# One float32 comparison for both one-hot sets of the gate rows, and a written TensorE order in block 2

## The chip, the cores and the metric

The kernel runs on one core of a Trainium2 chip. The metric is the device time of one execution in microseconds (us). The engines are TensorE (PE, with its weight loads as PEld), VectorE (DVE), ScalarE (ACT), GpSimd (POOL) and SyncE (SP), which issues most of the transfers. Each engine works through its own instructions in a fixed order and waits on semaphores for the others.

## The reference, cut to what matters

The program is two transformer blocks over 512 tokens of 1024 channels, in float32. The first is a hybrid attention layer, which the change does not touch. The second has a token mixer (here called block 2) and a PEER layer:

```
p = xn @ w_in                      # 7 column groups: xa ga vb bb cb ma mb
ya = rg_lru(conv4(xa) + b) * gelu(ga)
yb = bb * conv3(cb * vb)
h  = h + (sigmoid(ma) * ya + sigmoid(mb) * yb) @ w_out
...
idx, g = top-16 of 256 candidates, for 8 heads and each token   # 128 experts of 16384
act = gelu(u[idx] . xn);   out = sum over the 128 of g * act * v[idx]
```

rg_lru has two gates, each a 128x128 matmul per head on the convolved xa, and a scan over the tokens.

## The kernel before

**Numbers.** Large matmuls are done as three: weights and inputs are split into a high part (a cast by ACT, `whi`, `xhi`) and the rest (a subtraction, `wlo`, `xlo`), and hi*hi, lo*hi and hi*lo are summed in PSUM. A weight block of 128 columns is loaded by SP (`wraw`), cast by ACT and subtracted by POOL or DVE; each of the three has a ring of 3.

**Block 2** (`block2`) runs over 8 blocks of 128 channels. Each takes seven tiles of 24 matmuls, in the order xa, ga, vb, bb, cb, ma, mb, which `next_tile` makes and which alternate between two PSUM buffers (`mm`). The first three tiles of the first block (`ahead`) are made at the end of block 1, while its sums come in. `scaled` multiplies a tile by the row of norms `rb` on DVE, which also empties the PSUM buffer. From xa comes the convolution `xc` (one ACT and three DVE operations), split into `xch` and `xcl`, on which `gates` does twice three matmuls (`pr`, `pi`). Their tanh leads by ACT, DVE and POOL to the scan `hs`. At the end `mhi` and `mlo` hold the merged channels, and eight output tiles over `wo2` (k is a channel block) are added to the residual `mo` (the variable `xr`). `RmsSum` takes their squares: `add` sums them on DVE and, for the last two, gives them to PE as matmuls with a column of ones (`st`).

The order of each engine's instructions is set by the scheduler of the framework from its own estimates. The code's order is a preference only.

**Gate rows** (`gate_matrix`). Token group 0 is done by gathering rows. For the groups 1, 2 and 3 (`DT`) all 16384 experts are computed densely, and a matrix of gates is needed: for each token, row (128) by column (128) of the expert number. Per 128 tokens, indices and weights are transposed on PE (`gt`), the index is cut in two 7-bit halves (`hi_`, `iT`), and then for each 4 tokens: two DVE comparisons make one-hot rows in bfloat16,

```
eq = R.tile([128, 2, 128, 4], BF16, name="eq", bufs=2)
for e in range(2):
    V.tensor_tensor(out=eq[:, e], in0=iota, in1=iT[:, e, None, t:t + 4].to_broadcast([128, 128, 4]),
                    op=OP.is_equal)
```

ACT copies the first set to float32 (`A`), POOL multiplies the second by the weights (`B`), PE multiplies the two for each of the 4 tokens in float32 (`gp`, 4 matmuls, 8 records in the trace), and ACT copies the result to `stage`. 8 such groups of 4 tokens make one transfer of 2 MB to `gd` in DRAM; 3 x 128 tokens are 96 groups.

**Around it.** `u_step` loads a block of 128 rows of u, splits it and multiplies it with the 384 tokens (`ups`, 24 matmuls), DVE scales it (`act`), ACT takes the gelu. 11 of these are written into `peer_query`, the others into `peer_experts`, and the scheduler pulls some of them among the gate rows. After the gate rows `peer_experts` goes through all 128 blocks: remaining u steps, gates read back (`gate<-gd`), and 18 matmuls for v (`acc`).

Of the kernel before, what the change touches and what calls it, by code (L numbers as in the profile page):

```python
# [6 lines left out]
F32 = mybir.dt.float32  # L7
# [10 lines left out]
KD = 8  # L18
# [747 lines left out]
def block2(g, xr):  # L766

    nc, tc = g.nc, g.tc
    V = nc.vector
    with ExitStack() as ctx:  # L770
        P = ctx.enter_context(tc.tile_pool(name="b2", bufs=1, reuse_waits="tile"))
        R = ctx.enter_context(tc.tile_pool(name="b2r", bufs=2, reuse_waits="tile"))
        pb = g.pg
# [12 lines left out]
        def next_tile():  # L786
            return ahead.pop(0) if ahead else emit_tile()

        mhi = P.tile([128, 8, T], F32R, name="mhi")
        mlo = P.tile([128, 8, T], F32R, name="mlo")  # L790
        def scaled(nm, out=None, half=False):
            t = out if out is not None else R.tile([128, T], F32, name=nm)
            if half:
                V.scalar_tensor_tensor(t, next_tile(), 0.5, rb, op0=OP.mult, op1=OP.mult)
            else:
                V.tensor_tensor(out=t, in0=next_tile(), in1=rb, op=OP.mult)
            return t

        for i in range(8):
# [18 lines left out]
            def gates(o, e):  # L818
                for j, (w, x) in enumerate(((wah, xch), (wal, xch), (wah, xcl))):
                    nc.tensor.matmul(o, w[:, e, :], x, start=j == 0, stop=j == 2)  # L820

            gates(pr, 0)
            tr = t("tr")
            nc.scalar.activation(tr, pr, AF.Tanh, scale=0.5, bias=bh[:, i:i + 1])
# [15 lines left out]
            hs = t("hs", "xc")  # L840
            V.tensor_tensor_scan(hs, av, ti, 0.0, op0=OP.mult, op1=OP.add)

            ga = scaled("ga")
            g2 = t("g2")
            nc.scalar.activation(g2, ga, AF.Square)
            V.tensor_scalar(out=g2, in0=g2, scalar1=GC, scalar2=1.0, op0=OP.mult, op1=OP.add)
# [2 lines left out]
            V.scalar_tensor_tensor(g2, g2, 1.0, ga, op0=OP.add, op1=OP.mult)  # L849
            nc.gpsimd.tensor_tensor(out=hs, in0=hs, in1=g2, op=OP.mult)  # L850

            vb = scaled("vb")
            bb = scaled("bb")
            cb = R.tile([128, 2 + T], F32, name="cb")
            nc.gpsimd.memset(cb[:, 0:2], 0.0)
# [18 lines left out]

        g.xhi, g.xlo, g.rb, g.rtok = operands(g)
        st = RmsSum(g, R, "pt")
        for k in range(KD):
            ps = proj_tile(g, wblock(g, g.a["wo2"][k]), mhi, mlo)
            V.tensor_tensor(out=xr[:, k, :], in0=ps, in1=xr[:, k, :], op=OP.add)
            scaled_split(g, g.xhi, g.xlo, xr, "n2", [k])  # L880
            st.square(xr[:, k, :])
            st.add()
        st.finish(g.rb, g.rtok)


# [6 lines left out]
GPAD = 128  # L892
NEXP = 128
RUN = 32
GB = 3
ULO = 10
NROW = 4
SMH = 4
# [127 lines left out]
def gate_matrix(g, gd):  # L1026

    nc, tc = g.nc, g.tc
    V = nc.vector
    nb = 0  # L1030
    with tc.tile_pool(name="peg", bufs=2, reuse_waits="tile") as R:
        iota = R.tile([128, 128, 4], BF16, name="iota", bufs=1)
        nc.gpsimd.tensor_copy(iota, g.cst[:, C_IOTA:C_IOTA + 128, None].to_broadcast([128, 128, 4]))
        for m, tt in enumerate(DT):
            ps = g.pg.tile([128, 512], F32, name="gt", tag="pg")
            nc.tensor.transpose(ps[:, 0:128], g.idxf[:, tt, :], g.ident)
            nc.tensor.transpose(ps[:, 128:256], g.wgt[:, tt, :], g.ident)
            ii = R.tile([128, 128], I32, name="ii", bufs=1)
            V.tensor_copy(ii, ps[:, 0:128])
            wT = R.tile([128, 128], F32, name="wT")  # L1040
            nc.scalar.copy(wT, ps[:, 128:256])
            hi_ = R.tile([128, 2, 128], I32, name="hi_", bufs=1)
            V.tensor_scalar(out=hi_[:, 0, :], in0=ii, scalar1=7, scalar2=None, op0=OP.logical_shift_right)
            V.tensor_scalar(out=hi_[:, 1, :], in0=ii, scalar1=127, scalar2=None, op0=OP.bitwise_and)
            iT = R.tile([128, 2, 128], BF16, name="iT")
            V.tensor_copy(iT, hi_)
            for b in range(128 // TB):
                stage = R.tile([128, 128, TB], F32, name="stage")
                for q in range(TB // 4):
                    t = b * TB + q * 4  # L1050
                    eq = R.tile([128, 2, 128, 4], BF16, name="eq", bufs=2)
                    for e in range(2):
                        V.tensor_tensor(out=eq[:, e], in0=iota, in1=iT[:, e, None, t:t + 4].to_broadcast([128, 128, 4]),  # L1053
                                        op=OP.is_equal)
                    A = R.tile([128, 4, 128], F32, name="A", bufs=GB)
                    nc.scalar.copy(A, eq[:, 0].rearrange("p i t -> p t i"))
                    B = R.tile([128, 4, 128], F32, name="B", bufs=GB)
                    nc.gpsimd.tensor_tensor(out=B, in0=eq[:, 1].rearrange("p i t -> p t i"),
                                            in1=wT[:, t:t + 4, None].to_broadcast([128, 4, 128]), op=OP.mult)
                    ps = g.pg.tile([128, 512], F32, name="gp", tag=("pg", "pt")[q % 2])  # L1060
                    for j in range(4):
                        nc.tensor.matmul(ps[:, j * 128:(j + 1) * 128], B[:, j, :], A[:, j, :], start=True, stop=True)
                    nc.scalar.copy(stage[:, :, q * 4:q * 4 + 4], ps.rearrange("p (t i) -> p i t", t=4))
                nc.sync.dma_start(gd[nb, :, :128 * TB], stage.rearrange("p i t -> p (i t)"))
                nb += 1
# [149 lines left out]
```

## Time and profile before

| | |
|---|---|
| median of 3 runs | 2197.82 us (2194.63 to 2198.39) |
| the profiled execution | 2196.98 us, its span 2195.2 us |
| PE busy | 2078.9 us of the span, 95% |
| DVE busy | 1570.0 us, 72% |
| POOL busy | 1004.3 us, 46% |
| ACT busy | 901.9 us, 41% |

The stages are read from the span's start: block 1 to 458 us, block 2 to 835 (its output tiles from 781), queries and top-16 to 1035, gate rows to 1195, experts to 2195. A busy PE is not a PE at its best pace, since the ends of matmuls are modelled; where PE waits, the waits tell more than the busy share.

### The profile page before, as it was taken

What the parts mean: (1) busy time and instruction counts of PE and PEld (TensorE: products, weight loads), DVE (VectorE), ACT (ScalarE), POOL (GpSimd) and SP (SyncE); (2) the same over time, 40 slices, a digit from 0 to 9 for tenths busy, and PEclk for the clock granted to TensorE, in tenths of its full rate; (3) what the DMA queues carried; (4) which work ended last, traced back from release to release, by engine and by line L of the source; (5) the groups of instructions that cost most, each with busy time, mean ns of one, the idle gap of its engine ahead of it and who ended that gap; (6) DMA issues with size and microseconds to landing.
All of it is one profiled execution on the core that took longest, in us unless ns stands there. A gap on an engine that the chain in (4) does not pass through costs nothing.

```text
span 2195.2 us, 29184 instructions
## 1 busy us (share of the span) xinstructions
PE 2078.9 (95%) x10582; PEld 1789.8 (82%) x10582; DVE 1570.0 (72%) x2759; ACT 901.9 (41%) x1436; POOL 1004.3 (46%) x835
## 2 busy tenths in 40 slices
PE   8999998899999999797888999999999999999998
PEld 6777786677777777677767999999999999999886
DVE  5534546266766756999997798788787888888674
ACT  4434433344444433333776333333333333333333
POOL 3534341545665645764665144444444444443220
PEclk9999999999999999999999999999999999999999
DMA  4111111212232233222444998889989988888573
GB/s 154 49 38 49 57 65 53 96 58 87 87 96 87 87 90 111 69 71 74 174 166 185 335 359 303 307 294 313 304 298 305 313 301 298 305 312 285 182 261 105
DMA packets 147153, 394.09 MB, mean 180 GB/s; under 512 B 11585, under 2 KB 60865, under 8 KB 145217
## 3 DMA queue, kind: packets, MB, share of 16 engines
q1 hardware_dynamic: 110144, 258.00, 35.2%
q0 software_dynamic: 36864, 134.23, 17.6%
q8 instruction: 83, 1.36, 0.3%
q14 instruction: 62, 0.50, 0.1%
HBM read 364.92 MB, written 27.26 MB: 179 GB/s over the span
## 4 chain that ended last, share of the span: by engine, by line
PE 44%; DVE 13%; issue 2%; DMA 1%; POOL 1%; ACT 1%; SPq 0%; POOLq 0%; DVEq 0%; ACTq 0%
PE acc L1169 23%; PE ups L219 19%; DVE eq L1053 5%; DMA gate<-gd 1%; DVE t L1021 1%; DVE idxf L992 1%; DVE ind L1023 1%; POOL pr L988 1%; DVE ind L1020 1%; DVE eq L984 1%; DVE val L1022 1%; DVE val L1019 1%; DVE cand L963 0%; DVE act L912 0%; DVE wlo L195 0%
## 5 line engine op out<-in xcount | busy, mean ns | idle before, releaser
L194 ACT CAST whi<-wraw 128x1024 fp32r<-128x1024 f32 x248 | 260.4, 1050 | 499.0 <-PE ups L219 295.0
L195 POOL TENSOR_TENSOR wlo<-wraw,whi 128x1024 fp32r<-128x1024 f32 x127 | 307.4, 2425 | 247.3 <-ACT whi L194 241.5
L1090 POOL DMA_INDIRECT row<-u,idx x128 | 198.6, 1551 | 272.1 <-DVE row L1096 233.5
L1090 POOL DMA_INDIRECT row<-v,idx x128 | 182.2, 1424 | 279.5 <-DVE xtok L1108 266.7
L219 PE MATMUL mm<-xhi,whi 128*128 128x512 f32 x856 | 234.8, 406 | 3.6 <-ACT xhi L194 3.6
L1169 PE MATMUL acc<-vhi,cl 128*128 128x512 f32 x768 | 237.6, 390 | 0.0
L1169 PE MATMUL acc<-vlo,ch 128*128 128x512 f32 x768 | 237.0, 389 | 0.4 <-DVE vlo L195 0.4
L1169 PE MATMUL acc<-vhi,ch 128*128 128x512 f32 x768 | 237.1, 389 | 0.0
L219 PE MATMUL mm<-xhi,wlo 128*128 128x512 f32 x856 | 237.0, 408 | 0.0
L219 PE MATMUL mm<-xlo,whi 128*128 128x512 f32 x856 | 231.5, 401 | 0.0
L219 PE MATMUL ups<-xhi,whi 128*128 128x384 f32 x1024 | 205.0, 339 | 6.3 <-DVE best L1019 4.9
L219 PE MATMUL ups<-xhi,wlo 128*128 128x384 f32 x1024 | 201.7, 336 | 0.0
L219 PE MATMUL ups<-xlo,whi 128*128 128x384 f32 x1024 | 201.0, 335 | 0.0
L219 PEld LDWEIGHTS ups<-xhi,whi 128*128 128x128 f32 x1024 | 181.4, 189 | 16.6 <-issue 7.6
L219 PEld LDWEIGHTS mm<-xhi,wlo 128*128 128x128 f32 x856 | 162.7, 195 | 37.6 <-issue 5.1
L219 PEld LDWEIGHTS mm<-xlo,whi 128*128 128x128 f32 x856 | 159.3, 191 | 35.4 <-issue 4.9
L219 PEld LDWEIGHTS mm<-xhi,whi 128*128 128x128 f32 x856 | 158.5, 192 | 36.3 <-ACT xhi L194 4.0
L195 DVE TENSOR_TENSOR wlo<-wraw,whi 128x1024 fp32r<-128x1024 f32 x121 | 149.3, 1234 | 53.9 <-ACT whi L194 53.9
L219 PEld LDWEIGHTS ups<-xhi,wlo 128*128 128x128 f32 x1024 | 180.5, 189 | 0.0
L219 PEld LDWEIGHTS ups<-xlo,whi 128*128 128x128 f32 x1024 | 179.3, 188 | 0.0
L194 ACT CAST ch<-act 128x384 fp32r<-128x384 f32 x128 | 65.6, 514 | 275.3 <-PE acc L1169 275.3
L1169 PEld LDWEIGHTS acc<-vlo,ch 128*128 128x128 f32 x768 | 144.1, 188 | 30.9 <-DVE vlo L195 0.9
(456 smaller groups left out, 3628.8 us busy)
## 6 DMA issues: line engine op xcount, KB each, us to landing
wraw<-uT SPq DMA_DIRECT2D x128, 512.0 KB
vring<-v SPq DMA_DIRECT2D x128, 512.0 KB
wraw<-w SPq DMA_DIRECT2D x88, 512.0 KB
gd<-stage SPq DMA_DIRECT2D x12, 2048.0 KB
gate<-gd SPq DMA_DIRECT2D x32, 768.0 KB
wraw<-wo SPq DMA_DIRECT2D x16, 512.0 KB
wraw<-wq SPq DMA_DIRECT2D x16, 512.0 KB
xr<-xT SPq DMA_DIRECT2D x8, 256.0 KB
```

What stands on the lines that cost most here:

```text
L194: nc.scalar.copy(hi, src)
L195: return (lo_eng or nc.vector).tensor_tensor(out=lo, in0=src, in1=hi.bitcast(F32), op=OP.subtract)
L219: nc.tensor.matmul(out, w(k), x(k), start=j == 0, stop=j == len(ps) - 1)
L984: V.tensor_tensor(out=eq[:, :n], in0=rank[:, :n], in1=pf[:, q].rearrange("p t k -> p (t k)")[:, None, :].to_broadcast([128, n, 16]), op=OP ...
L988: nc.gpsimd.tensor_tensor(out=pr[:, :n].rearrange("p c (t k) -> p c t k", t=4), in0=eq[:, :n].rearrange("p c (t k) -> p c t k", t=4), in1= ...
L992: V.tensor_reduce(out=g.idxf[:, :, h * 16 + 4 * q:h * 16 + 4 * q + 4], in_=pr[:, :n].rearrange("p c (t k) -> p t k c", t=4), axis=AX.X, op ...
L1019: V.max(out=v[:, 0:8], in_=x)
L1020: V.max_index(out=i[:, 0:8], in_max=v[:, 0:8], in_values=x)
L1021: V.match_replace(out=y[:, :n], in_to_replace=v[:, 0:8], in_values=x, imm_value=-3.0e38)
L1053: V.tensor_tensor(out=eq[:, e], in0=iota, in1=iT[:, e, None, t:t + 4].to_broadcast([128, 128, 4]), op=OP.is_equal)
L1090: nc.gpsimd.indirect_dma_start(out=r, out_offset=None, in_=g.a[tab], in_offset=bass.IndirectOffsetOnAxis(ap=s.idx[:, i:i + 1], axis=0))
L1169: nc.tensor.matmul(acc[m][e], l[:, ts], r[:, e * 512:(e + 1) * 512], start=False, stop=end and l is cl)
```

## The change

In `gate_matrix` the column numbers are written once by PE into a PSUM tile (`iota`, from the `mm` ring), as a float32 product with the identity. The index halves `iT` are float32. One DVE comparison over 128x1024 elements makes both sets of one-hots in float32 (`oh`, a ring of 4, `GB`). POOL multiplies the second half by the weights in place. PE reads both halves from `oh`. The copies by ACT are gone. In `block2` the order of PE is the order of the code (`manual_schedule`), the tiles ga and vb with their scaling come before the gates, the first two output tiles do k = 0 to 6 of both and then k = 7 of both, and `st.add` stands one output tile later.

```diff
@@ block2
+        ctx.enter_context(tc.manual_schedule(engines={mybir.EngineType.PE}))
...
+            ps_ga = next_tile()
+            ga = scaled("ga", ps=ps_ga)
+            ps_vb = next_tile()
+            vb = scaled("vb", ps=ps_vb)
             gates(pr, 0)
...
-            ga = scaled("ga")
...
-            vb = scaled("vb")
             bb = scaled("bb")
...
         st = RmsSum(g, R, "pt")
+        w = [wblock(g, g.a["wo2"][k]) for k in range(2)]
+        first = [g.pmm.tile([128, 512], F32, name="mm", tag="mm") for k in range(2)]
+        for ks in (range(KD - 1), [KD - 1]):
+            for (h_, l_), ps in zip(w, first):
+                ops = [(wt, x, k) for wt, x in ((h_, mhi), (l_, mhi), (h_, mlo)) for k in ks]
+                for j, (wt, x, k) in enumerate(ops):
+                    nc.tensor.matmul(ps, wt[:, k, :], x[:, k, :], start=k == 0 and j == 0, stop=k == KD - 1 and j == 2)
         for k in range(KD):
-            ps = proj_tile(g, wblock(g, g.a["wo2"][k]), mhi, mlo)
+            ps = first[k] if k < 2 else proj_tile(g, wblock(g, g.a["wo2"][k]), mhi, mlo)
+            if k:
+                st.add()
             V.tensor_tensor(out=xr[:, k, :], in0=ps, in1=xr[:, k, :], op=OP.add)
             scaled_split(g, g.xhi, g.xlo, xr, "n2", [k])
             st.square(xr[:, k, :])
-            st.add()
+        st.add()
         st.finish(g.rb, g.rtok)
...
-GB = 3
+GB = 4
@@ gate_matrix
-        iota = R.tile([128, 128, 4], BF16, name="iota", bufs=1)
-        nc.gpsimd.tensor_copy(iota, g.cst[:, C_IOTA:C_IOTA + 128, None].to_broadcast([128, 128, 4]))
+        iota = g.pmm.tile([128, 512], F32, name="iota", tag="mm").rearrange("p (t i) -> p t i", t=4)
+        nc.tensor.matmul(iota, g.ident, g.cst[:, None, C_IOTA:C_IOTA + 128].to_broadcast([128, 4, 128]), start=True, stop=True)
...
-            iT = R.tile([128, 2, 128], BF16, name="iT")
+            iT = R.tile([128, 2, 128], F32, name="iT")
...
-                    eq = R.tile([128, 2, 128, 4], BF16, name="eq", bufs=2)
-                    for e in range(2):
-                        V.tensor_tensor(out=eq[:, e], in0=iota, in1=iT[:, e, None, t:t + 4].to_broadcast([128, 128, 4]),
-                                        op=OP.is_equal)
-                    A = R.tile([128, 4, 128], F32, name="A", bufs=GB)
-                    nc.scalar.copy(A, eq[:, 0].rearrange("p i t -> p t i"))
-                    B = R.tile([128, 4, 128], F32, name="B", bufs=GB)
-                    nc.gpsimd.tensor_tensor(out=B, in0=eq[:, 1].rearrange("p i t -> p t i"),
-                                            in1=wT[:, t:t + 4, None].to_broadcast([128, 4, 128]), op=OP.mult)
+                    oh = R.tile([128, 2, 4, 128], F32, name="oh", bufs=GB)
+                    V.tensor_tensor(out=oh, in0=iota[:, None, :, :].to_broadcast([128, 2, 4, 128]),
+                                    in1=iT[:, :, t:t + 4, None].to_broadcast([128, 2, 4, 128]), op=OP.is_equal)
+                    nc.gpsimd.tensor_tensor(out=oh[:, 1], in0=oh[:, 1], in1=wT[:, t:t + 4, None].to_broadcast([128, 4, 128]),
+                                            op=OP.mult)
...
-                        nc.tensor.matmul(ps[:, j * 128:(j + 1) * 128], B[:, j, :], A[:, j, :], start=True, stop=True)
+                        nc.tensor.matmul(ps[:, j * 128:(j + 1) * 128], oh[:, 1, j, :], oh[:, 0, j, :], start=True, stop=True)
```

How the orders move is shown at three places. The first is PE at the start of block 2, behind the last matmul of the third prepared tile (`m_3486`). Before:

```order
L738 MATMUL m_3486<-xlo,whi 128x512
L219 MATMUL mm<-xhi,whi 128x512 x8
L219 MATMUL mm<-xhi,wlo 128x512 x8
L219 MATMUL mm<-xlo,whi 128x512 x6
L820 MATMUL pr<-xch,wah 128x512
L820 MATMUL pr<-xch,wal 128x512
L820 MATMUL pi<-xch,wah 128x512
L820 MATMUL pi<-xch,wal 128x512
L219 MATMUL mm<-xlo,whi 128x512 x2
L219 MATMUL mm<-xhi,whi 128x512 x2
L820 MATMUL pr<-xcl,wah 128x512
L820 MATMUL pi<-xcl,wah 128x512
```

And PE at the same place in the changed kernel:

```order
L738 MATMUL m_3486<-xlo,whi 128x512
L822 MATMUL pr<-xch,wah 128x512
L822 MATMUL pr<-xch,wal 128x512
L822 MATMUL pr<-xcl,wah 128x512
L822 MATMUL pi<-xch,wah 128x512
L822 MATMUL pi<-xch,wal 128x512
L822 MATMUL pi<-xcl,wah 128x512
L219 MATMUL mm<-xhi,whi 128x512 x8
```

The fourth tile (bb), of which most stood ahead of the gates, now stands behind them, and the third gate matmul is the first that needs `xcl`.

The second place is PE in the seventh channel block, where the numbers tell tiles apart: before, `mm_5349` is its xa tile and `mm_5419` its ga tile.

```order
L219 MATMUL mm_5349<-xhi_3462,whi_5345 128x512 x8
L219 MATMUL mm_5349<-xhi_3462,wlo_5346 128x512 x8
L219 MATMUL mm_5349<-xlo_3463,whi_5345 128x512 x8
L219 MATMUL mm_5419<-xhi_3462,whi_5415 128x512 x8
L219 MATMUL mm_5419<-xhi_3462,wlo_5416 128x512 x8
L219 MATMUL mm_5419<-xlo_3463,whi_5415 128x512 x6
L820 MATMUL pr_5380<-xch_5385,wah_5381 128x512
L820 MATMUL pr_5380<-xch_5385,wal_5382 128x512
L820 MATMUL pi_5394<-xch_5385,wah_5381 128x512
L820 MATMUL pr_5380<-xcl_5386,wah_5381 128x512
L820 MATMUL pi_5394<-xch_5385,wal_5382 128x512
L820 MATMUL pi_5394<-xcl_5386,wah_5381 128x512
```

In the changed kernel, in the same block, `mm_5397` is the ga tile and `mm_5430` the vb tile (the xa tile stands just ahead of these rows):

```order
L219 MATMUL mm_5397<-xhi_3462,wlo_5394 128x512 x8
L219 MATMUL mm_5397<-xlo_3463,whi_5393 128x512 x8
L219 MATMUL mm_5430<-xhi_3462,whi_5426 128x512 x8
L219 MATMUL mm_5430<-xhi_3462,wlo_5427 128x512 x8
L219 MATMUL mm_5430<-xlo_3463,whi_5426 128x512 x8
L822 MATMUL pr_5382<-xch_5387,wah_5383 128x512
L822 MATMUL pr_5382<-xch_5387,wal_5384 128x512
L822 MATMUL pr_5382<-xcl_5388,wah_5383 128x512
L822 MATMUL pi_5462<-xch_5387,wah_5383 128x512
L822 MATMUL pi_5462<-xch_5387,wal_5384 128x512
L822 MATMUL pi_5462<-xcl_5388,wah_5383 128x512
L219 MATMUL mm_5494<-xhi_3462,whi_5490 128x512 x8
```

The gates stand behind 48 matmuls that follow the xa tile, where they stood behind 22.

The third place is DVE at the change from the first to the second 128 tokens of the gate rows. Before:

```order
L1053 TENSOR_TENSOR eq<-iota,iT 128x512 x50
L912 TENSOR_TENSOR act<-ups,rb 128x384
L1053 TENSOR_TENSOR eq<-iota,iT 128x512 x6
L195 TENSOR_TENSOR wlo<-wraw,whi 128x1024
L1039 CAST ii<-gt 128x128
L1043 TENSOR_SCALAR hi__8861<-ii 128x128
L1044 TENSOR_SCALAR hi__8861<-ii 128x128
L1046 CAST iT<-hi__8861 128x256
L1053 TENSOR_TENSOR eq<-iota,iT 128x512 x8
```

And in the changed kernel, at the change from the second to the third 128 tokens, which is the same as from the first to the second:

```order
L1068 TENSOR_TENSOR oh<-iota,iT 128x1024 x32
L926 TENSOR_TENSOR act<-ups,rb 128x384 x2
L1054 CAST ii<-gt 128x128
L195 TENSOR_TENSOR wlo<-wraw,whi 128x1024
L1058 TENSOR_SCALAR hi__9044<-ii 128x128
L1059 TENSOR_SCALAR hi__9044<-ii 128x128
L195 TENSOR_TENSOR wlo<-wraw,whi 128x1024
L1061 CAST iT<-hi__9044 128x256
L1068 TENSOR_TENSOR oh<-iota,iT 128x1024 x32
```

The 64 comparisons of 128 tokens are 32, with nothing among them, and what the u steps need of DVE (two `act`, two `wlo`) stands between the token groups.

## Rows read from the trace of the kernel before

**Rows 1.** Busy time by stretch: us, then engines, granted clock, DMA share, GB/s
```profile
458.00:781.00 323.00, 306.81 (x1321) 249.80 (x1321) 214.29 (x189) 143.94 (x181) 194.04 (x113) 0.98 0.28 88
...
1035.00:1195.00 160.00, 130.51 (x885) 110.95 (x884) 153.01 (x211) 118.36 (x204) 104.31 (x96) 0.99 0.40 162
1195.00:2145.00 950.00, 948.67 (x4825) 863.88 (x4825) 748.68 (x976) 341.62 (x463) 381.73 (x257) 1.00 0.88 297
```
**Rows 2.** Groups of instructions, 1028 to 1200 us: busy us, mean ns, idle before
```profile
L1053 DVE TENSOR_TENSOR eq<-iota,iT 128x512 bf16<-128x512 bf16 x192 | 142.9, 817 | 0.3
L1062 PE MATMUL gp<-A,B 128*128 128x128 f32 x768 | 112.2, 290 | 29.5 <-POOL B L1058 29.3
L1058 POOL TENSOR_TENSOR B<-eq,wT 128x512 f32<-128x512 bf16 x96 | 104.3, 1087 | 59.6 <-DVE eq L1053 59.6
```
**Rows 3.** Timeline of POOL in the gate rows: start us, us, idle before
```profile
1106.31 1.07 POOL L1058 TENSOR_TENSOR B<-eq,wT 128x512 f32<-128x512 bf16 x1 [0.45 <-DVE eq L1053]
1107.83 1.07 POOL L1058 TENSOR_TENSOR B<-eq,wT 128x512 f32<-128x512 bf16 x1 [0.46 <-DVE eq L1053]
```
**Rows 4.** The tile iota: ns min/median/max, first and last start us
```profile
L1053 DVE TENSOR_TENSOR eq<-iota,iT x192: 409/422/1290, 1035.3 to 1190.4; 128x512 bf16<-128x512 bf16 x192
```
**Rows 5.** Timeline at block 2's start: DVE operations on a PSUM tile
```profile
457.16 0.69 DVE L796 TENSOR_TENSOR ca<-mm,rb 128x512 f32<-128x512 f32 x1 [3.19 <-PE mm L738]
...
457.79 0.69 DVE L796 TENSOR_TENSOR ga<-mm,rb 128x512 f32<-128x512 f32 x1
```
**Rows 6.** Line 195 on DVE: ns min/median/max, first and last start us
```profile
L195 DVE TENSOR_TENSOR vlo<-vring,vhi x128: 1212/1220/1226, 1207.3 to 2179.5; 128x1024 fp32r<-128x1024 f32 x128
```
**Rows 7.** Groups of instructions of POOL, the whole span
```profile
L453 POOL TENSOR_TENSOR it<-it,cst 128x512 f32<-128x512 f32 x4 | 5.1, 1286 | 1.8 <-DVE it L452 1.8
```
**Rows 8.** Timeline in block 2: a DVE operation on a PSUM tile beside POOL
```profile
728.02 4.75 POOL L195 TENSOR_TENSOR wlo<-wraw,whi 128x1024 fp32r<-128x1024 f32 x2
...
729.22 0.69 DVE L857 TENSOR_TENSOR cb<-mm,vb 128x512 f32<-128x512 f32 x1 [1.94 <-PE mm L219]
```
**Rows 9.** Timeline of PE in the gate rows
```profile
1092.29 1.16 PE L1062 MATMUL gp<-A,B 128*128 128x128 f32 x8 [0.36 <-POOL B L1058]
1093.21 0.77 PE L219 MATMUL ups<-xhi,whi 128*128 128x384 f32 x3
1093.82 1.16 PE L1062 MATMUL gp<-A,B 128*128 128x128 f32 x8
```
**Rows 10.** Waits of PE, 455 to 840 us: us in total, times, longest
```profile
PE pr L820 <- ACT xch L194: 13.1, 8, 3.2
PE pr L820 <- DVE xcl L195: 3.1, 1, 3.1
PE mm L219 <- ACT mhi L872: 2.3, 1, 2.3
PE st L283 <- DVE sacc L280: 1.5, 1, 1.5
```
**Rows 11.** Busy time by stretch in block 2 (columns as in rows 1)
```profile
460.00:480.00 20.00, 15.89 (x57) 12.19 (x56) 15.25 (x13) 8.71 (x13) 12.78 (x9) 0.83 0.32 106
500.00:520.00 20.00, 17.21 (x69) 14.07 (x70) 14.63 (x14) 9.94 (x13) 10.32 (x7) 0.91 0.21 75
```
**Rows 12.** Timeline at block 2's start: the last prepared matmul, and xcl
```profile
458.06 0.40 PE L738 MATMUL m<-xlo,whi 128*128 128x512 f32 x1
...
466.81 2.83 DVE L195 TENSOR_TENSOR xcl<-xc,xch 128x512 fp32r<-128x512 f32 x1
```
**Rows 13.** Timeline in the seventh channel block: from xa's scaling to xcl
```profile
704.93 0.68 DVE L796 TENSOR_TENSOR ca<-mm,rb 128x512 f32<-128x512 f32 x1
...
710.60 0.69 DVE L195 TENSOR_TENSOR xcl<-xc,xch 128x512 fp32r<-128x512 f32 x1 [0.68 <-ACT xch L194]
```
**Rows 14.** Timeline of DVE at the change to the second 128 tokens
```profile
1082.11 2.79 DVE L1053 TENSOR_TENSOR eq<-iota,iT 128x512 bf16<-128x512 bf16 x3
...
1088.70 5.35 DVE L1053 TENSOR_TENSOR eq<-iota,iT 128x512 bf16<-128x512 bf16 x8
```

More of the change, by code (lines that the diff above doesn't have):

```diff
@@ L790, in block2, with scaled @@
         mlo = P.tile([128, 8, T], F32R, name="mlo")
-        def scaled(nm, out=None, half=False):
+        def scaled(nm, out=None, half=False, ps=None):
             t = out if out is not None else R.tile([128, T], F32, name=nm)
+            ps = next_tile() if ps is None else ps
             if half:
-                V.scalar_tensor_tensor(t, next_tile(), 0.5, rb, op0=OP.mult, op1=OP.mult)
+                V.scalar_tensor_tensor(t, ps, 0.5, rb, op0=OP.mult, op1=OP.mult)
             else:
-                V.tensor_tensor(out=t, in0=next_tile(), in1=rb, op=OP.mult)
+                V.tensor_tensor(out=t, in0=ps, in1=rb, op=OP.mult)
             return t
```

## The prediction

> **What bounds the kernel now.** I read the busy time by stretch first, then the stretches that the change touches: the groups of the gate rows and their timeline, and PE's waits in block 2. The stretch by stretch view shows two regimes [rows 1]. From 1195 us to 2145 PE is busy 948.67 of 950 us: the experts are PE work without gaps, so a stretch ahead that gets shorter moves the end by as much, as long as the transfers follow. In the gate rows PE is busy 130.5 of 160 us and DVE 153.0, and in block 2 PE is busy 306.8 of 323. These two have something to give.
>
> In the gate rows 96 groups follow each other. The groups show PE waiting 29.3 us for POOL's `B`, and POOL waiting 59.6 us for DVE's `eq`, while DVE hardly ever waits (0.3 us) [rows 2]. The timeline of POOL is a strict beat: 1106.31, 1107.83, so 1.52 us a group, of which 1.07 is POOL at work and 0.45 its wait for `eq` [rows 3]. The reader is to see that DVE is busy but not at its own pace: the median comparison takes 422 ns, the longest 1290, the mean 817 [rows 2, 4]. One comparison of each pair runs while POOL rests, the other is held while POOL works. POOL's 1.07 and one free comparison add up to the beat, as if the two engines shared one door.
>
> **The gate rows, part by part.** ACT's copy to `A` goes; ACT is not waited for there, so I count nothing. DVE's two comparisons become one of 1024 elements in float32, one operand in PSUM. The trace has 512 elements from PSUM at 0.69 us, the next starting 0.63 after the first [rows 5], and 1024 elements between two SBUF operands at 1.22 us [rows 6]. So the new one takes 1.22 us, and following ones start at least 1.16 apart (0.06 of overlap, as in rows 5). POOL's multiplication keeps its 512 elements but reads float32: between 1.07 us, as now, and the 1.29 us of an operation on two float32 operands [rows 2, 7]. PE's four matmuls follow each other in 0.92 us, and three u matmuls take 0.61 [rows 9], 0.2 each.
>
> Does the door close again? An operation of DVE that reads one operand from PSUM ran its usual 0.69 us in the middle of 4.75 us of POOL's subtractions [rows 8], so I take the two engines to run side by side. The beat is then the longest of DVE (1.16 to 1.22), POOL (1.07 to 1.29) and PE. In the changed order of PE about a third of the groups have one or two u matmuls behind them: 0.92 + 1.6 x 0.2 = 1.24. I take 1.22 for all, nearest to DVE's row; the bounds are 1.165 and 1.34 (POOL's 1.29 and 0.05 between two of them).
>
> Between two sets of 128 tokens DVE has more to do than before. Now 3.8 us pass from the end of the third comparison of a run (1084.9) to the next one (1088.70) [rows 14], with one `wlo` among it. In the changed order two `act` and a second `wlo` come in. The extra is under 0.7 + 1.2 us, partly in place of the wait for `gt`, so I take 5.0 us, twice.
>
> Now the first and the last comparison start 155.1 us apart [rows 4]. Then it is 95 x 1.22 + 2 x 5.0 = 125.9. The drain behind the last one is alike (a POOL and a PE step). That is 29.2 us less. Besides, the changed order has 115 u matmuls among the gate matmuls and 54 ahead of them, against 93 and 58: 18 more, at 0.2 each 3.6 us that the expert stage no longer has to do. Gate rows: -32.8.
>
> At this point a rule speaks against the change. The Trainium skill (VectorE: DVE Perf Modes, The perf-mode tier table) gives `tensor_tensor` a double pace for bfloat16 in SBUF and the plain pace for float32 or any PSUM operand. The trace agrees: 422 ns and 0.69 us for 512 elements [rows 4, 5]. By that rule alone a group goes from 0.84 us of DVE work to 1.22 and the stage gets 36 us longer. It would, if DVE ran at that pace now; the beat of 1.52 says that it does not.
>
> **Block 2, part by part.** PE waits there for `xch` 8 times, 13.1 us together, once for `xcl` 3.1, once for `mhi` 2.3 and once for the sum of squares 1.5 [rows 10]. Behind the two long waits, at the start, the granted clock has a mean of 0.83 and 0.91 over 20 us [rows 11], that is stretches at 1.2 instead of 2.4 GHz, which lose 3.4 and 1.8 us. All of it is 25.2 us.
>
> In the blocks after the first the gates need `xcl` 6.4 us after the scaling of xa began (704.93 to 711.29) [rows 13]. A tile of 24 matmuls is 24 x 306.8 / 1321 = 5.6 us [rows 1]. Before, 22 matmuls covered that chain, now two tiles, 11.1 us: the wait goes, and there are over 3 us to spare for a DVE that is late. What is late next is the chain behind the gates (tanh, reciprocal, scan on DVE), which starts one tile later than it did and stands on DVE ahead of the scaling of bb and cb. PE needs the buffer of bb two tiles after bb starts, and I count no wait, but this is the thinnest place.
>
> At the start it is the other way. The three prepared tiles end at 458.5 (458.06 + 0.40), and nothing covers the chain to `xch` and `xcl` any more, since the bb tile now stands behind the gates. `xcl` was there at 469.64 [rows 12], after 2.83 us where it mostly takes 0.69 [rows 13]. In the changed order one DVE operation less stands in front of it. I take 466 for its end, so 7.5 us of idle PE, and 2.5 us for the lower clock behind it (between the 1.8 and 3.4 above): 10.0 us. The bounds are 8 and 14.5 (xcl at 469.6, 3.4 us of clock).
>
> The wait for `mhi` goes: 42 matmuls of k = 0 to 6 stand in its place, 9.8 us. The wait for squares goes with the tile's delay. New is that both first output tiles end within 0.7 us, so that the third waits for DVE's addition: 0.4 us. Sum of block 2: -25.2 + 10.0 + 0.4 = -14.8.
>
> **Sum.** The profiled execution took 2196.98 us, 0.8 below the median of the runs. 2197.0 - 32.8 - 14.8 = 2149.4; I say 2150.
>
> **Rivals.**
>
> POOL sets the beat. For it speaks the 1.29 us of POOL's float32 multiplication of that size [rows 7]; against it, that `B` with the same broadcast weights takes 1.07 [rows 3]. At 1.34 a group the stage is 95 x 0.12 = 11.4 us longer than in the forecast: 2161.
>
> The door stays shut. The new comparison still reads `iT` from SBUF. If that operand or the 4 KB of output goes by the way that POOL needs, each group is one after the other, 1.16 + 1.07 = 2.23 us: 95 x 1.01 = 96 us more than forecast, 2246, slower than before. It decides from a beat of 1.7 on. Against it stands the operation from PSUM beside POOL [rows 8]. The Trainium skill (SBUF — State Buffer, Who interferes with whom) says too that a DVE instruction with at most one SBUF input, outside the two-port modes, does not contend with GpSimd; the trace agrees with its 0.69 us.
>
> Block 2 gives nothing. If the scaling of bb or cb comes 1.5 us too late in each of 8 blocks and the start costs 14.5 us, the gains there are used up: 2164. For it speaks that POOL and DVE do the chain behind the gates with little slack; against it, that DVE is busy only 214 of 323 us [rows 1].
>
> The transfers don't follow. The gate matrix (24 MB) is written in a fifth less time, and the DMA share is already 0.88 over the experts [rows 1]. If PE then waits 10 us for u, v or gates: 2160.
>
> **How the numbers follow.** Forecast 0.60, its own range 2140 to 2158; POOL's beat 0.16; block 2 without gain 0.12; transfers 0.08; the door 0.04. The lower end is DVE's 1.165 (-5.2), a start at 8 (-2) and a change of token sets at its present 3.8 (-2.4), so 2140, and 2138 with u matmuls better placed; the upper end holds POOL's beat together with half of block 2's gain: 2169. I give 2138 to 2170. A measurement of this kernel tells 0.2% (4.4 us) from no change. All cases but the door are faster by more than that: faster 0.95, same 0.01, slower 0.04.
>
> **What would show it.** In the changed profile: `oh` 96 times at about 1.22 us with one duration (two durations, or 2.2 us, would be the door); its starts 1.17 to 1.25 apart; POOL's multiplication between 1.07 and 1.29 us, with idle time in front of it if DVE sets the beat and none if POOL does; PE's waits for `xch` gone but for the first channel block, where one of 5 us or more stands, with a lowered clock behind it; no wait of PE for a DVE scaling at the tiles ma and mb; the expert stretch still over 99% busy. I am wrong if the beat is above 1.35, or if PE in block 2 waits in every channel block.

## The result and the profile after

The changed kernel takes 2143.08 us (median of 4 runs, 2141.64 to 2144.91), the kernel before 2198.11 beside it: a ratio of 0.975, 95% interval 0.9732 to 0.9768. That is 55 us less, 7 below the forecast of 2150 and inside its range. The profiled execution took 2143.05 us, its span 2141.3.

Busy time by stretch, columns as in [rows 1], whose stretches these are in the changed kernel:

```profile
458.00:781.00 323.00, 311.92 (x1351) 253.78 (x1350) 236.15 (x192) 146.13 (x184) 195.35 (x114) 0.98 0.28 90
...
1020.00:1145.00 125.00, 124.54 (x929) 116.45 (x928) 122.66 (x122) 66.05 (x113) 99.97 (x96) 1.00 0.52 210
1145.00:1195.00 50.00, 48.72 (x298) 48.43 (x297) 28.50 (x45) 17.65 (x23) 5.75 (x4) 1.00 0.99 340
1195.00:2095.00 900.00, 899.62 (x4524) 814.93 (x4524) 720.21 (x932) 323.54 (x439) 376.73 (x253) 1.00 0.87 296
```

The gate rows fit into 125 us instead of 160, and PE is now busy 124.54 of them. The experts still have no gaps, and in the 50 us between, where the transfers fill 0.99, PE loses 1.3, in one wait for DVE (the kernel before lost 1.1 in the 50 us behind its gate rows):

```profile
PE ups L219 <- DVE act L926: 1.3, 1, 1.3
```

The one-hot sets, to be held against [rows 2 to 4]:

```profile
L1074 PE MATMUL gp<-oh x768: 270/275/377, 1026.1 to 1143.7; 128*128 128x128 f32 x192
L1068 DVE TENSOR_TENSOR oh<-iota,iT x96: 1210/1210/1225, 1023.6 to 1140.5; 128x1024 f32<-128x1024 f32 x96
L1070 POOL TENSOR_TENSOR oh<-oh,wT x96: 1040/1041/1044, 1025.0 to 1141.8; 128x512 f32<-128x512 f32 x96
```

Minimum, median and maximum agree on both engines. Nothing is held any more: the comparison of [rows 4] ran from 409 to 1290 ns. DVE's timeline, over a run of 32 comparisons and at the change to the second 128 tokens [rows 14]:

```profile
1023.62 36.29 DVE L1068 TENSOR_TENSOR oh<-iota,iT 128x1024 f32<-128x1024 f32 x32
1059.83 1.01 DVE L926 TENSOR_TENSOR act<-ups,rb 128x384 f32<-128x384 f32 x2
...
1064.50 36.29 DVE L1068 TENSOR_TENSOR oh<-iota,iT 128x1024 f32<-128x1024 f32 x32
```

32 comparisons take 36.29 us, so they start (36.29 - 1.21) / 31 = 1.132 apart. The beat was 1.52 [rows 3]. Between two runs 4.6 us pass (1059.91 to 1064.50).

PE's waits in block 2, to be held against [rows 10], and PE's timeline at its start [rows 12]:

```profile
PE pr L822 <- ACT xch L194: 6.3, 1, 6.3
PE pr L822 <- DVE xcl L195: 3.1, 1, 3.1
PE mm L219 <- DVE bb L798: 1.7, 5, 0.4
```

```profile
459.49 0.40 PE L738 MATMUL m<-xlo,whi 128*128 128x512 f32 x1
466.21 0.79 PE L822 MATMUL pr<-xch,wah 128*128 128x512 f32 x1 [6.32 <-ACT xch L194]
466.81 0.63 PE L822 MATMUL pr<-xch,wal 128*128 128x512 f32 x1
470.51 0.79 PE L822 MATMUL pr<-xcl,wah 128*128 128x512 f32 x1 [3.08 <-DVE xcl L195]
```

The waits of the later blocks for `xch`, and those for `mhi` and for the squares, are gone; those of the first block have grown to 9.4 us, and the granted clock there is lower than it was [rows 11]:

```profile
460.00:480.00 20.00, 10.71 (x35) 8.15 (x36) 16.22 (x13) 8.38 (x14) 10.68 (x8) 0.74 0.24 80
```

On DVE two operations there are far over their usual 1.22 and 0.69 us, while POOL works:

```profile
465.43 2.28 DVE L195 TENSOR_TENSOR wlo<-wraw,whi 128x1024 fp32r<-128x1024 f32 x1
467.64 2.82 DVE L195 TENSOR_TENSOR xcl<-xc,xch 128x512 fp32r<-128x512 f32 x1
```
```profile
464.92 1.71 POOL L853 TENSOR_TENSOR g<-g,ga 128x512 f32<-128x512 f32 x1
466.59 3.32 POOL L195 TENSOR_TENSOR wlo<-wraw,whi 128x1024 fp32r<-128x1024 f32 x1
```

DVE's `wlo` ends at 467.71, 1.08 us behind POOL's `g` (466.63), and `xcl` at 470.46, 0.55 behind POOL's `wlo` (469.91). The experiment iota_sbuf shows what these distances mean.

**A ledger for all kernels.** Five marks cut every profiled execution: DVE's `ms` (the sum of squares is complete) at the end of block 1 and again at the end of block 2, the first and the last comparison of the gate rows, and the end of the span. For the changed kernel the first two are

```profile
L291 DVE TENSOR_SCALAR ms<-st x1: 163/163/163, 455.2 to 455.2; 128x4 f32<-128x4 f32 x1
```
```profile
L291 DVE TENSOR_SCALAR ms<-st x1: 149/149/149, 825.4 to 825.4; 128x4 f32<-128x4 f32 x1
```

The columns are the stretches between the marks in us, then the median of the runs and its ratio to the kernel before on the same chip.

| kernel | block 1 | block 2 | queries | gate rows | rest | median | ratio (95%) |
|---|---|---|---|---|---|---|---|
| before | 453.8 | 381.8 | 199.7 | 155.1 | 1004.8 | 2198.11 | 1 |
| changed | 455.2 | 370.2 | 198.2 | 116.9 | 1000.8 | 2143.08 | 0.975 (0.9732-0.9768) |
| gate_only | 453.8 | 381.7 | 199.8 | 116.8 | 1001.1 | 2154.75 | 0.9812 (0.9784-0.9841) |
| block2_only | 456.9 | 370.0 | 197.0 | 155.7 | 1005.2 | 2184.05 | 0.9942 (0.9922-0.9962) |
| bf16_psum | 450.9 | 370.3 | 198.1 | 133.6 | 999.8 | 2157.33 | 0.9828 (0.9799-0.9858) |
| iota_sbuf | 454.3 | 369.5 | 198.1 | 197.4 | 1001.6 | 2224.90 | 1.0126 (1.0101-1.015) |
| no_pool | 455.7 | 381.7 | 199.7 | 106.4 | 1010.5 | 2155.32 | 0.9797 (0.9775-0.9819) |
| two_ops | 452.4 | 370.2 | 198.1 | 123.6 | 1000.5 | 2150.14 | 0.9778 (0.9759-0.9797) |
| ring3 | 453.6 | 370.1 | 198.2 | 125.6 | 1000.0 | 2149.51 | 0.9785 (0.9759-0.9812) |
| one_tile | 453.3 | 376.8 | 198.7 | 116.8 | 999.7 | 2151.51 | 0.9794 (0.9768-0.982) |
| wo2_plain | 453.4 | 377.9 | 197.7 | 116.9 | 999.5 | 2149.05 | 0.9784 (0.9758-0.981) |
| bb_first | 459.4 | 364.7 | 197.5 | 116.8 | 999.3 | 2139.46 | 0.9715 (0.9696-0.9734) |
| bc_first | 454.0 | 361.6 | 197.6 | 116.9 | 999.5 | 2132.39 | 0.9701 (0.9681-0.9721) |
| bc_spare | 452.1 | 361.7 | 197.2 | 116.9 | 999.5 | 2137.38 | 0.9726 (0.9704-0.9747) |

Block 1 is the same in all of them and still ends anywhere from 450.9 to 459.4. A part that was not touched repeats within some tenths in block 2 and in the gate rows. So for a few us the stretches say more than the medians. From before to changed the spans differ by 53.9: +1.4 block 1, -11.6 block 2, -1.5 queries, -38.2 gate rows, -4.0 the rest.

### The profile page after: what moved, and what is told of

It is laid out like the page before. It is cut to its first block, busy times and chain, and to the rows that moved or that the text cites. A ratio compares the mean times of both kernels' runs of the same rounds, so it can differ in the third digit from the quotient of the medians.

```text
span 2141.3 us, 28911 instructions
## 1 busy us (share of the span) xinstructions
PE 2059.9 (96%) x10584; PEld 1783.5 (83%) x10584; DVE 1553.5 (73%) x2663; ACT 845.9 (40%) x1340; POOL 1000.3 (47%) x834
## 4 chain that ended last, share of the span: by engine, by line
PE 51%; DVE 8%; POOL 1%; DMA 1%; issue 1%; ACT 0%; POOLq 0%; DVEq 0%; SPq 0%; ACTq 0%
PE acc L1181 24%; PE ups L219 22%; PE gp L1074 4%; DVE t L1035 1%; DVE idxf L1006 1%; POOL pr L1002 1%; DVE ind L1037 1%; DVE ind L1034 1%; DVE eq L998 1%; DVE val L1036 1%; DMA gate<-gd 1%; DVE val L1033 1%; DVE cand L977 0%; DVE wlo L195 0%; DVE pos L1037 0%
## 5 line engine op out<-in xcount | busy, mean ns | idle before, releaser
L195 POOL TENSOR_TENSOR wlo<-wraw,whi 128x1024 fp32r<-128x1024 f32 x127 | 312.7, 2468 | 225.4 <-ACT whi L194 222.6
L219 PE MATMUL mm<-xlo,whi 128*128 128x512 f32 x856 | 226.9, 397 | 0.0
```

What stands on the lines that cost most here:

```text
L195: return (lo_eng or nc.vector).tensor_tensor(out=lo, in0=src, in1=hi.bitcast(F32), op=OP.subtract)
L219: nc.tensor.matmul(out, w(k), x(k), start=j == 0, stop=j == len(ps) - 1)
```

## The experiments

**Each part alone.** gate_only has block 2 of the kernel before, block2_only its gate rows.

```diff
 # gate_only, and all else that the change did in block2
-        ctx.enter_context(tc.manual_schedule(engines={mybir.EngineType.PE}))
...
 # block2_only, and all else that the change did in gate_matrix
-GB = 4
+GB = 3
...
```

> Only the gate rows are changed, block 2 is as before. Theory (the two parts add up): the traces give the gate rows 155.1 to 116.9 us from the first to the last comparison, and 4.0 us less behind the last, so 42.2 of the 55 us: 2156, between 2153 and 2159. Rival (the parts depend on each other, the expert stage or the lower clock takes some of it): 2162 or more, and then block 2 alone must gain over 14 us.

> Only block 2 is changed, the gate rows are as before. Theory (the two parts add up): from the last prepared tile to the norm of the next stage the traces are 11.6 us apart, so 2186.5, between 2184 and 2189. The prediction's own term was -14.8, which would be 2183. Rival (the written order in block 2 only shifts the waits into the queries and the gate rows): 2194 or more.

Measured: 0.9812 and 0.9942. Their product is 0.9755, the changed kernel's 0.975, and stretch by stretch each part alone gives what it gives in both (116.8 and 116.9, 370.0 and 370.2). The parts add up; both rivals fall.

**Does POOL hold the comparison?** First POOL is taken away from the gate rows of the kernel before.

```diff
-                    B = R.tile([128, 4, 128], F32, name="B", bufs=GB)
-                    nc.gpsimd.tensor_tensor(out=B, in0=eq[:, 1].rearrange("p i t -> p t i"),
-                                            in1=wT[:, t:t + 4, None].to_broadcast([128, 4, 128]), op=OP.mult)
...
-                        nc.tensor.matmul(ps[:, j * 128:(j + 1) * 128], B[:, j, :], A[:, j, :], start=True, stop=True)
+                        nc.tensor.matmul(ps[:, j * 128:(j + 1) * 128], A[:, j, :], A[:, j, :], start=True, stop=True)
```

> The kernel before, without POOL's multiplication in the gate rows; PE multiplies the first set with itself, so the gates and all that follows from them are other numbers. The two bfloat16 comparisons and their SBUF operands are as they were. Theory (POOL held every second comparison): all 192 take about 0.42 us, none over 0.7; the beat falls from 1.52 to what ACT needs for its two copies, about 1.27, the stage from 155 to about 131 us: 2171. Rival (the long ones are DVE's own, from waiting for the ring or from the operands' form): about half of them stay at 0.8 to 1.3 us.

The tile `iota` there (ns minimum, median, maximum, then first and last start):

```profile
L1053 DVE TENSOR_TENSOR eq<-iota,iT x192: 412/419/427, 1037.1 to 1143.5; 128x512 bf16<-128x512 bf16 x192
```

All 192 take 412 to 427 ns. The long ones of [rows 4] were POOL's doing. The beat is 106.4 / 95 = 1.12, lower than I expected: I had added up ACT's two copies, but they overlap. The time, 2155, missed the expected 2171 by that, less the 5.7 us by which the rest is longer. What holds that stage is ACT, as expected: DVE waits for its copy `A`, and ACT, which waits only 0.2 us for PE's `gp`, is busy 104.75 of 107 us. PE is busy all the time too, but by ends that are modelled (columns of the second row as in [rows 1]):

```profile
DVE eq L1053 <- ACT A L1056: 21.1, 59, 0.8
```
```profile
1037.00:1144.00 107.00, 106.92 (x854) 101.39 (x853) 79.03 (x209) 104.75 (x198) 0.00 (x0) 1.00 0.59 239
```

**Does it matter where the column numbers stand?** The old form with the numbers in PSUM, and the new form with the numbers in SBUF.

```diff
 # bf16_psum: gate rows of before, with
-        iota = R.tile([128, 128, 4], BF16, name="iota", bufs=1)
-        nc.gpsimd.tensor_copy(iota, g.cst[:, C_IOTA:C_IOTA + 128, None].to_broadcast([128, 128, 4]))
+        iota = g.pmm.tile([128, 512], F32, name="iota", tag="mm").rearrange("p (i t) -> p i t", t=4)
+        nc.tensor.matmul(iota, g.ident, g.cst[:, C_IOTA:C_IOTA + 128, None].to_broadcast([128, 128, 4]), start=True, stop=True)
 # iota_sbuf: the changed kernel with
-GB = 4
+GB = 3
+        iota = R.tile([128, 4, 128], F32, name="iota", bufs=1)
+        nc.gpsimd.tensor_copy(iota, g.cst[:, None, C_IOTA:C_IOTA + 128].to_broadcast([128, 4, 128]))
```

> Block 2 as changed; the gate rows in their old form (two bfloat16 comparisons, copy by ACT, multiplication from bfloat16 by POOL, a ring of 3), with one edit: the column numbers stand in PSUM. Theory (POOL held the comparison because both its operands came from SBUF): every comparison takes 0.69 us, with no long ones, the two of a group 0.63 apart, 1.26 a group; the stage falls from 155 to about 131 us: 2162, between 2158 and 2168. Rival (where the numbers stand is nothing, the single wide operation brought the gain): one of each pair stays held behind POOL's 1.07 and the beat is 1.07 + 0.63 = 1.70: 2204. What could lie in between: ACT, with its copy of A and of stage, about 1.2 us a group.

> The changed kernel with one edit: the column numbers in float32 in SBUF, written once by POOL, instead of PSUM (and the ring of oh 3 instead of 4, for its room). Theory (door): the comparison of 1024 and POOL's multiplication take turns, 1.13 + 1.04 = 2.17 us a group, 95 x 1.04 = 99 us more: 2242, slower than the kernel before; some comparisons then show about 2.2 us. Rival (the plain pace and the single operation are all of it): 1.13 to 1.2 a group as now, 2143 to 2150.

The comparisons of bf16_psum:

```profile
L1067 DVE TENSOR_TENSOR eq<-iota,iT x192: 679/681/693, 1019.3 to 1152.9; 128x512 bf16<-128x512 f32 x192
```

And of iota_sbuf, with POOL's multiplication and a piece of both timelines:

```profile
L1068 DVE TENSOR_TENSOR oh<-iota,iT x96: 1218/1741/2071, 1021.9 to 1219.3; 128x1024 f32<-128x1024 f32 x96
L1070 POOL TENSOR_TENSOR oh<-oh,wT x96: 1032/2016/2106, 1023.3 to 1221.9; 128x512 f32<-128x512 f32 x96
```
```profile
1105.21 1.74 DVE L1068 TENSOR_TENSOR oh<-iota,iT 128x1024 f32<-128x1024 f32 x1 [0.24 <-PE gp L1074]
1107.19 1.74 DVE L1068 TENSOR_TENSOR oh<-iota,iT 128x1024 f32<-128x1024 f32 x1 [0.24 <-PE gp L1074]
```
```profile
1103.86 21.81 POOL L1070 TENSOR_TENSOR oh<-oh,wT 128x512 f32<-128x512 f32 x11
```

With PSUM alone the old form runs every comparison in 0.68 us, slower than the free 0.42 and yet 22.1 us faster over the stage than block2_only, from which it differs by this one edit (155.7 to 133.6). The expected stage was 131, and the time, 2157.33, lies just below its range. With SBUF, and a ring of 3 that alone costs 8.7 us (ring3, below), the new form needs 197.4 us, more than the old one. The place of one operand decides, and the single wide operation without it would have made the kernel slower.

The size was off, +80.5 us where 99 were expected. Both engines' operations are longer than when nothing holds them (DVE 1.74 instead of 1.21, POOL 2.02 instead of 1.04), and they lie side by side in the timeline. Their ends show turns all the same: 85 of the 96 comparisons end 1.079 to 1.084 us behind the end of a multiplication, and 88 of the 96 multiplications 0.895 to 0.901 behind the end of a comparison. In the rows above the first comparison ends at 1106.95, 1.08 behind a multiplication that began at 1103.86 and took 2.02. So the time for which one waits for the other stands inside its own duration, and a turn is some 0.13 to 0.14 us shorter than the operation alone (1.08 for 1.21, 0.90 for 1.04). 1.08 + 0.90 = 1.98 is the beat, which POOL without a gap shows as 21.81 / 11; the expectation had taken 1.13 and 1.04 for the turns.

The kernel before shows the same: 92 comparisons are held there and end 0.279 to 0.287 us behind POOL's multiplication, 0.14 less than the 0.42 of a free one. And so do the two long operations at the start of block 2 (1.08 for 1.22, 0.55 for 0.69). The Trainium skill (SBUF — State Buffer, Who interferes with whom) says that a DVE instruction with two SBUF inputs contends with a GpSimd one that reads SBUF, and one with at most one, outside the two-port modes, does not; the traces agree with both halves.

**What are the single operation and the fourth buffer worth?**

```diff
 # two_ops
-                    V.tensor_tensor(out=oh, in0=iota[:, None, :, :].to_broadcast([128, 2, 4, 128]),
-                                    in1=iT[:, :, t:t + 4, None].to_broadcast([128, 2, 4, 128]), op=OP.is_equal)
+                    for e in range(2):
+                        V.tensor_tensor(out=oh[:, e], in0=iota, in1=iT[:, e, t:t + 4, None].to_broadcast([128, 4, 128]),
+                                        op=OP.is_equal)
 # ring3
-GB = 4
+GB = 3
```

> The changed kernel with two float32 comparisons of 512 a group in place of one of 1024; the rest is the same (column numbers in PSUM, no copy by ACT, ring of 4). Theory (DVE sets the beat): 2 x 0.63 = 1.26 us a group where it is 1.13, 95 x 0.13 = 12 us: 2155, between 2152 and 2158. Rival (PE sets it: it is busy 124.5 of 125 us in that stage): fewer u matmuls fit there in any case, the beat grows by less than 0.05: 2143 to 2148.

> The changed kernel with a ring of 3 for the one-hot sets instead of 4. Theory (each set is used up about 2.5 us after its comparison began, so three are enough at a beat of 1.13): no difference, 2141 to 2145. Rival (DVE runs ahead of PE within a run of 32 and needs the fourth): DVE waits for PE in the stage, 2147 or more.

two_ops: the stage is 6.7 us longer, between the two expectations. The comparisons are 0.677 us each, and the 64 of the first 128 tokens stand in one row:

```profile
1020.70 38.35 DVE L1069 TENSOR_TENSOR oh<-iota,iT 128x512 f32<-128x512 f32 x64
```

So they start (38.35 - 0.68) / 63 = 0.60 apart, 1.20 a group, and not the 0.63 of [rows 5]. DVE sets the beat, as the theory said.

ring3: my expectation was wrong, the stage grows by 8.7 us. In the changed kernel the first set is compared at 1023.62 (above), multiplied and used up at

```profile
1025.01 5.48 POOL L1070 TENSOR_TENSOR oh<-oh,wT 128x512 f32<-128x512 f32 x5 [9.51 <-DVE oh L1068]
```
```profile
1026.11 1.16 PE L1074 MATMUL gp<-oh 128*128 128x128 f32 x8
```

so it lives 1027.27 - 1023.62 = 3.65 us, not the 2.5 that I had guessed. Three buffers allow 3.65 / 3 = 1.22 a group, four 0.91. In ring3 DVE's starts are (31.78 - 1.21) / 25 = 1.223 apart, and behind some of them it waits for PE:

```profile
1029.27 31.78 DVE L1068 TENSOR_TENSOR oh<-iota,iT 128x1024 f32<-128x1024 f32 x26
...
1069.61 3.49 DVE L1068 TENSOR_TENSOR oh<-iota,iT 128x1024 f32<-128x1024 f32 x3 [0.59 <-PE gp L1074]
```

1.22 is also one comparison without any overlap, but the starts tell the two apart. Of the 87 comparisons with three sets ahead of them in their own 128 tokens, 75 start 0.105 to 0.108 us after PE's last matmul on the set three before has ended. The one at 1029.27 above follows these, which end at 1029.16:

```profile
1028.00 1.16 PE L1074 MATMUL gp<-oh 128*128 128x128 f32 x8
```

The ring sets the beat: a set lives 3.56 us there in the median, and (3.56 + 0.11) / 3 = 1.22.

**The two covers in block 2.** one_tile puts the vb tile behind the gates again (from the second block on); wo2_plain makes the first two output tiles one after the other.

```diff
 # one_tile
-            ps_vb = next_tile()
-            vb = scaled("vb", ps=ps_vb)
             gates(pr, 0)
...
             gates(pi, 1)
+            ps_vb = next_tile()
+            vb = scaled("vb", ps=ps_vb)
 # wo2_plain, and without the loop over first
-            ps = first[k] if k < 2 else proj_tile(g, wblock(g, g.a["wo2"][k]), mhi, mlo)
+            ps = proj_tile(g, wblock(g, g.a["wo2"][k]), mhi, mlo)
```

> The changed kernel with the vb tile put behind the gates from the second channel block on, so that one tile of 24 matmuls stands between xa and the gates where there are two; the written order, the output tiles and the gate rows are as changed. Theory (the chain to xch and xcl takes 6.4 us, one tile covers 5.6): PE waits for xch about 1 us and for xcl some 0.4 in each of 7 blocks, the waits for bb of 1.7 go: 2143 + 8 = 2151, between 2148 and 2155. Rival (the written order by itself is what removed the waits): 2146 or less.

> The changed kernel with the first two output tiles of block 2 made one after the other, all 8 channel blocks in turn, as the other six; the sum of squares stays one tile later. Theory (the 42 matmuls of the first seven blocks cover the chain to the last mhi): PE waits for mhi from 777.7, after 7 matmuls, to 783.3, 5.6 us, with some 2 us of lower clock behind it: 2143 + 7.5 = 2150.5, between 2148 and 2153. Rival (that chain has little to do with it, since the scheduler's order before lost only 2.3): 2146 or less.

PE's waits in block 2, of one_tile and of wo2_plain:

```profile
PE pr L822 <- ACT xch L194: 13.5, 8, 6.3
PE pr L822 <- DVE xcl L195: 3.1, 1, 3.1
```
```profile
PE pr L822 <- ACT xch L194: 6.3, 1, 6.3
PE mm L219 <- ACT mhi L877: 5.5, 1, 5.5
PE pr L822 <- DVE xcl L195: 3.1, 1, 3.1
PE mm L219 <- DVE bb L798: 1.7, 5, 0.4
```

one_tile brings 7.2 us of waits for `xch` back in seven blocks and loses those for `bb`; block 2 is 6.6 us longer. wo2_plain waits 5.5 for `mhi`, and block 2 is 7.7 longer. Both are as the theory had them, but for the 0.4 us a block for `xcl`, which did not come: what stands in front of the wait makes the gain, not that the order is written.

**The start of block 2.** bb_first makes the bb tile of the first channel block ahead of its gates; bc_first bb and cb with their DVE operations; bc_spare takes another PSUM bank for bb besides.

```diff
 # bb_first
+            ps_bb = next_tile() if i == 0 else None
             gates(pr, 0)
...
-            bb = scaled("bb")
+            bb = scaled("bb", ps=ps_bb)
 # bc_first (b_and_c holds the five lines from bb to cb)
+            if i == 0:
+                bb, cb = b_and_c()
             gates(pr, 0)
...
+            if i:
+                bb, cb = b_and_c()
 # bc_spare, besides
+    ps = g.pg.tile([128, 512], F32, name="m3", tag="pt") if spare else g.pmm.tile([128, 512], F32, name="mm", tag="mm")
...
+                bb = scaled("bb", ps=next_tile(i > 0))
```

> The changed kernel with the bb tile of the first channel block made ahead of its gates, as it stood before (all other blocks as changed). Theory (the start of block 2 costs PE 9.4 us of waits and about 3 of lower clock): 24 matmuls, 5.6 us, fill the wait of 6.3 for xch; 0.7 of it stays, and the 3.1 for xcl: 2143 - 5.6 - 1 = 2136.5, between 2135 and 2139. Rival (what ends last there is the chain on DVE, so PE then waits for the scaling of bb instead): 2141 to 2144, with a new wait for bb of 4 us or more in the first block.

> As the kernel with the bb tile first, but bb and cb of the first channel block both stand, with their DVE operations, ahead of its gates: 48 matmuls, 11.1 us, behind the prepared tiles. Theory (cover is all that lacks): the waits for xch and xcl of 6.3 and 3.1 go, and the lower clock behind them too: 2143 - 9.4 - 2.5 = 2131, between 2129 and 2134. Rival (DVE then does bb and cb ahead of xcl and the chain behind the gates is late): a wait for xcl or for ma stays, 2136 or more.

> As the kernel with bb and cb of the first channel block ahead of its gates, and from the second block on the bb tile is written into a PSUM bank of another ring that is idle there, so that the ma tile no longer waits for the scaling of bb. Theory: the five waits for bb, 3.7 us with one of 2.4, and the granted clock of 0.91 over 20 us behind the long one (1.8 us) go: 2132 - 5.5 = 2127, between 2125 and 2130. Rival (DVE is late there anyway, so the mb tile or the next gates wait in its place): 2131 to 2134.

PE's waits in block 2, of bb_first, bc_first and bc_spare:

```profile
PE pr L822 <- DVE xcl L195: 3.6, 1, 3.6
PE mm L219 <- DVE bb L798: 1.7, 5, 0.4
PE pr L822 <- ACT xch L194: 0.9, 1, 0.9
```
```profile
PE mm L219 <- DVE bb L798: 3.7, 5, 2.4
```
```profile
PE mm L219 <- DVE cb L834: 5.7, 7, 2.6
```

bb_first: block 2 is 5.5 us shorter than in the changed kernel, the tile's 5.6 (the median is 2139.46, just above the range given, with block 1 4.2 us later in the profile). bc_first: 8.6 shorter, not 11.9. The waits at the start are gone, but DVE, which now does bb and cb first, is late with `bb` in the second block, and the granted clock falls there:

```profile
460.00:480.00 20.00, 20.00 (x90) 16.50 (x89) 19.85 (x15) 11.28 (x17) 17.38 (x12) 1.00 0.42 132
...
500.00:520.00 20.00, 17.58 (x71) 14.05 (x70) 14.10 (x11) 8.97 (x12) 12.75 (x9) 0.91 0.24 79
```

Its rival held in part. bc_spare's rival held for the stage: without the wait for `bb` PE waits for `cb`, and block 2 stays at 361.7. DVE, which makes both, is late there. The median, 2137.38, lies above both ranges, though no stretch but block 1 differs from bc_first's by more than 0.4 us; its runs lie between 2129.19 and 2140.78, so they show no gain, and don't show that it is slower. bc_first beats both kernels: 2132.39 us, 0.9701 (0.9681 to 0.9721), an interval clear of the changed kernel's.

## Why the prediction was right

- **The door**, the way into SBUF that the prediction has DVE and POOL share, was read rightly: POOL's multiplication held the comparison (no_pool), an operand in PSUM ends that (bf16_psum), and without it the change loses (iota_sbuf, 1.0126). The rule against the change, DVE's plain pace in float32, is true too: 1.21 us for 1024. It did not decide, since DVE had not been running at its pace. Were the door shut, the price would be 1.98 a group, not 2.23: the turns add up, not the operations.
- **The gate rows, mis-sized**: -29.2 forecast, -38.2 measured. The failed step is "I take 1.22 for all". DVE's comparisons lie 1.132 apart, below the bound of 1.165, since one takes 1.21 and neighbours overlap by 0.08, where 1.22 and 0.06 were taken. The 1.24 of PE's mixed groups was no beat: within the sets of 128 tokens 53 of 93 groups have no u matmul behind them and 40 have one or two, 65 in all, so the mean is 0.92 + 65 x 0.2 / 93 = 1.06. The fourth buffer bridges the rest: where PE falls behind, a set lives up to 4.34 us, and (4.34 + 0.11) / 4 = 1.11 is still under DVE's 1.13. With three the 1.22 came true. 95 x 0.09 is 8.4 us, the changes of token sets (4.6, not 5.0) are the rest.
- **POOL's beat** did not come: 1.04 us, below the range of 1.07 to 1.29. Reading bfloat16 beside comparisons on PSUM it takes as long (1.047 in bf16_psum), so float32 cost it nothing.
- **u matmuls**: -3.6 forecast, -4.0 measured behind the last comparison.
- **Block 2, mis-sized the other way**: -14.8 forecast, -11.6 measured. The start has 9.4 us of waits, not 7.5, since `xcl` again took 2.82 us, as in [rows 12], and a `wlo` of 2.28 stood ahead of it: the door that the prediction found in the gate rows, and did not look for here. The thinnest place gave: five waits for `bb`, 1.7 us. The third output tile's 0.4 did not come. 1.9 + 1.7 - 0.4 = 3.2 is as much as the whole difference. The clock's part is less sure: in block 2 PE is busy 9.5 us at 1.2 GHz before and 5.7 after. Half of that is lost, 4.8 and 2.8 us (an estimate from the two traces), so 1.9 came back and not 5.2 - 2.5 = 2.7. Waits and clock then make 10.8; where the other 0.8 us come from stays open.
- **The transfers** followed: they fill 0.99 of 50 us behind the gate rows, as they filled all of 50 us before, and PE's one wait there is for DVE.
- Not forecast: the queries 1.5 us shorter, which goes with the change in block 2 (197.0 in block2_only, 199.8 in gate_only), and block 1, which is not touched, 1.4 longer. -9.0 - 0.4 + 3.2 - 1.5 + 1.4 = -6.3, from 2149.4 to the 2143.05 of the profiled execution. That the gate rows and block 2 missed in opposite directions, and so partly cancel, is luck.

## What to carry to other kernels

Where an operation's durations come in two sizes, look for the engine that works during the long ones; moving one operand to PSUM can be worth more than DVE's faster pace, even when it costs that pace. An operation's duration can hold its wait for another engine: the distances between their ends show the turns. Compute the beat of a ring from the life of one buffer over their number, and a mean over groups rather than its slowest kind. When a tile is moved ahead of a wait, ask whether the first round, which has nothing ahead of it, needs an order of its own.

## What the runs showed of the hardware

- Operations of DVE with two SBUF operands and operations of POOL took turns, and the wait stands inside the duration. A held operation ended 1.08 us (DVE, 1024 float32), 0.28 (DVE, 512 bfloat16) or 0.90 (POOL, 512 float32) behind the other engine's, 0.13 to 0.14 less than it takes alone. Beside bfloat16 comparisons DVE alone was held, up to 1290 ns, since POOL began its 1.07 us when DVE had made its set [rows 3, 4]; where both had work waiting both were longer, 1.74 and 2.02.
- POOL multiplied 512 float32 elements in place by weights that repeat along the innermost dimension in 1.04 us. By 128 constants repeated four times as a row it took 1.29 [rows 7], and with two full tiles as much (`hs` in block 2, 1.284 to 1.304).
- Following DVE operations on a PSUM operand start 0.08 us before the one ahead ends, with 512 elements as with 1024 (0.60 for 0.677, 1.132 for 1.21).
- The same instructions up to the end of block 1 took 450.9 to 459.4 us in fourteen profiled executions. What makes them differ was not tried.
